# The first RMS norm of a two-block kernel: squares summed on VectorE, root and reciprocal on one column per 128 tokens

## The chip, the cores and the metric

One core of one Trainium2 chip runs the whole program in one launch. The metric is the device time in microseconds (us), the median of several runs. The kernel is written in a tile language: the source says which instructions exist and which data they use, and a planner decides in which order each engine gets them, by its own estimates of when each will be ready. Semaphores between the engines follow from the data and from the reuse of buffers.

## The reference, cut to what matters

There are 512 tokens of 1024 features and two blocks. Only the head of the first block is touched:

```
def rms_norm(x, w):
    xf = x.astype(jnp.float32)
    y = xf * lax.rsqrt(jnp.mean(xf * xf, axis=-1, keepdims=True) + EPS)
    return (y * w.astype(jnp.float32)).astype(x.dtype)
...
mod = jax.nn.silu(c) @ w_mod[l] + b_mod[l]
shift, scale, gate = jnp.split(mod, 3, axis=-1)
u = rms_norm(h, norm_w[l]) * (1.0 + scale[:, None, :]) + shift[:, None, :]
p = u @ w_in[l]
```

Behind it come attention, a convolution branch (GLU, depthwise convolution of width 31, layer norm, pointwise matmul), and the second block (RWKV mixer, memory attention, feed-forward).

## The kernel before, in words

Features lie on the 128 partitions and tokens on the free axis, so `x` comes as eight tiles of 128x512 (`xs[0..7]`, tile name `x`). RMS norm needs the sum of squares over features, which is a sum over the eight tiles and over the partitions.

Before the change, ScalarE (ACT) squares each tile into one of the four `tA` buffers, and TensorE (PE) multiplies it by a 128x128 matrix of 1/1024 (`ones`) into the bank `pj` of PSUM, adding the eight up. Every partition of `pj` then holds the mean square of each token, 128x512. ACT takes the root into `bs`, VectorE (DVE) the reciprocal, in place, again 128x512.

PE starts with `WARM` = 12 matmuls on zeros of 128x512 bf16 (`warm_up`), which have no use but to keep it busy. An ACT function table is loaded by an instruction of its own (ACT_TABLE_LOAD) where the next function isn't in the one loaded; a one-column Sqrt on `th` stands behind the Tanh to have Sqrt's table in place early.

The modulation comes from `mod_group`: eight matmuls of 32 rows (`pj<-modw,c`, eight 32-column weight loads of `c`), a copy `tA<-pj` on ACT, small matmuls `pv<-g,tA` of 2 columns, and on DVE the additions `c<-pv` that give `shift` and `A1`. `mod_pair(g)` serves the feature tiles 2g and 2g+1; the pair 0 is done in two halves. The groups 4 and 5 give the gate.

The loop `for j in range(KT)` then makes tile j of `u` (`apply_mod`: DVE multiplies `x` by `bs` into `tA`, ACT applies `A1` and `shift` once into `U` as the high part and once into `tA`, DVE forms the low part `U`), splits the weight tile `wr` into `wh` (ACT) and `wl` (DVE), and adds 18 matmuls of 128x512 to six accumulators (`accs`: two double banks `s`, two banks `pt`). I call these 18 matmuls group j. The first four of a group need only the high part of `u`. All weights and `w_mod` come through one DMA queue in the order of the source; `wr` has 2 buffers, `wl` 2, `wh` 3, `modw` 10.

Behind the loop come GLU (`hg<-tA,s`, `hg<-tA,pt`), the gate groups (`c<-pv`, 128x4), the convolution as 120 DVE instructions `hg<-hg,c` of low priority, a further projection `pj<-U`, and q and k/v projections.

A class `SumSq` that the changed code calls existed before, and a helper `norm_bs` uses it for the 256 context tokens.

Of the kernel before, what the change touches and what calls it, by code (L numbers as in the profile page):

```python
# [12 lines left out]
F32R = mybir.dt.float32r  # L13
# [3 lines left out]
AF = mybir.ActivationFunctionType  # L17
# [5 lines left out]
P = 128  # L23
S = 512
D = 1024
KT = 8
# [120 lines left out]
def rest(k, src, hi, lo):  # L147
    return k.V.tensor_tensor(out=lo, in0=src, in1=hi.bitcast(F32), op=ALU.subtract)
# [32 lines left out]
def mm3(k, ps, wh, wl, ah, al, first, last):  # L181
    mm = k.T.matmul
    mm(ps, wh, ah, start=first, stop=False)
    mm(ps, wh, al, start=False, stop=False)
    k.mm = mm(ps, wl, ah, start=False, stop=last)
    return k.mm
# [80 lines left out]
def bcast(k, r, n, tag):  # L267
    b = k.t(tag)
    for j in range(n):
        k.T.transpose(b[:, j * P:(j + 1) * P], r[:, j:j + 1].to_broadcast([P, P]), k.ident)  # L270
    return b
# [65 lines left out]
MODW = 10  # L337
LATER = 1500
CTX = (0, 2)
WARM = 12  # L340
ZG = (1, 0, 1, 1, 1, 0, 0, 0, 0, 0, 0)

def block1(k, I, st, h1d):
    A, V, T, G, Y = k.A, k.V, k.T, k.G, k.Y
# [7 lines left out]
    def warm_up(n):  # L352
        ps = k.t("pj")
        for _ in range(n):
            T.matmul(ps, warm[:, 0:P], warm, start=True, stop=True)

    xs = []
# [5 lines left out]
    sc, th = k.cal([16]), k.cal([16])  # L363
# [2 lines left out]
    cc = k.cal([KT, 32])  # L366
    G.memset(cc, 0.0)
    V.tensor_scalar(out=cc[:, :, 0:2], in0=sc.rearrange("p (i j) -> p j i", i=2), scalar1=0.5, scalar2=None, op0=ALU.mult)
    A.activation(th[:, 0:1], th[:, 0:1], AF.Sqrt, scale=0.0, bias=k.eps[1e-6])

    mark = [None] * 3
    warm_up(WARM)
    shift, A1 = k.cal([2, KT]), k.cal([2, KT])
# [4 lines left out]
    def mod_load(g, i):  # L378
        t = k.t("modw", [2, S])
        Y.dma_start(out=t, in_=I["w_mod"][g, i])  # L380
        return t
# [14 lines left out]
    def mod_pair(g, ts, e0=0, e1=2):  # L396
        cols = mod_group(ts, e0, e1)
        for e in range(e0, e1):
            j = 2 * g + e
            V.tensor_scalar(out=shift[:, :, j], in0=cols[:, 2 * e, :], scalar1=k.vec("b_mod", j), scalar2=None, op0=ALU.add)  # L400
            V.tensor_scalar(out=A1[:, :, j], in0=cols[:, 2 * e + 1, :], scalar1=bm1[:, j:j + 1],
                            scalar2=k.vec("norm_w", j), op0=ALU.add, op1=ALU.mult)
# [15 lines left out]
    def apply_mod(x, w, bs, i, j, hi, lo, vec=False):  # L418
        t = k.t("tA", [w])
        mark[1] = V.tensor_tensor(out=t, in0=x, in1=bs, op=ALU.mult)  # L420
        a_ap, s_ap = A1[:, i, j:j + 1], shift[:, i, j:j + 1]
        A.activation(hi, t, AF.Identity, bias=s_ap, scale=a_ap)
        if vec:
            V.tensor_scalar(out=t, in0=t, scalar1=a_ap, scalar2=s_ap, op0=ALU.mult, op1=ALU.add)
        else:
            mark[2] = A.activation(t, t, AF.Identity, bias=s_ap, scale=a_ap)
        V.tensor_tensor(out=lo, in0=t, in1=hi.bitcast(F32), op=ALU.subtract)
        return hi, lo

    ones = k.cal([P])  # L430
    G.memset(ones, 1.0 / D)
    ps = k.t("pj")
    for j in range(KT):
        sq = k.t("tA")
        A.activation(sq, xs[j], AF.Square)
        T.matmul(ps, ones, sq, start=j == 0, stop=j == KT - 1)
    bs = k.t("bs")
    A.activation(bs, ps, AF.Sqrt, bias=k.eps[1e-6])
    V.reciprocal(out=bs, in_=bs)
    a0, a1 = k.t("s", [2, S]), k.t("s", [2, S])  # L440
    accs = [a0[:, 0, :], a0[:, 1, :], a1[:, 0, :], a1[:, 1, :], k.t("pt"), k.t("pt")]
    us = []
# [9 lines left out]
    def raw_load(j):  # L452
        raw = k.t("wr", [1024])
        Y.dma_start(out=raw[:, :768], in_=I["w_start"][j])
        raws.append(raw)
# [5 lines left out]
    for j in range(KT):  # L461
        raw, wh, wl = raws[j], k.t("wh", [1024], F32R), k.t("wl", [1024], F32R)
        A.activation(wh[:, :768], raw[:, :768], AF.Copy)
        if j < 2:
            mod_pair(0, mods[0], j, j + 1)
        elif j % 2 == 0:
            mod_pair(j // 2, mods[j // 2])
        u = apply_mod(xs[j], S, bs, 0, j, k.t("U", dt=F32R), k.t("U", dt=F32R))
        us.append(u)
        rest(k, raw[:, :768], wh[:, :768], wl[:, :768])  # L470
        if j + 2 < KT:
            raw_load(j + 2)
        if j % 2 == 0 and j // 2 + 2 < 6:
            mods.append([mod_load(j // 2 + 2, i) for i in range(4)])
        for m in range(6):
            c = slice(m * P, (m + 1) * P)
            mm3(k, accs[m], wh[:, c], wl[:, c], u[0], u[1], j == 0, j == KT - 1)
# [42 lines left out]
    for g in range(4):  # L520
        wh, wl = W1.next()
        for kk in range(2):
            j = 2 * g + kk
            c = slice(kk * S, (kk + 1) * S)
            for t in range(4):
                tt = slice(t * P, (t + 1) * P)
                uh, ul = us[j]
                ps = q_ps[t // 2][:, t % 2, :]
# [18 lines left out]
    for t in (2, 3, 4, 5, 0, 1):  # L547
        ps = k.t("pt", [256])
# [278 lines left out]
    for m in range(KT):  # L827
        if m % 2 == 0:
            wh, wl = W1.next()
        ps = oacc[m]  # L830
# [654 lines left out]
def emit(tc, I, out, dbg=None, stages=("b1", "b2", "ff")):  # L1485
    k = K(tc, dbg)
    nc = tc.nc
    with ExitStack() as st:
        k.open(st, "g", dict(g=1, wr=2, wh=3, wl=2))
        setup(k, I)  # L1490
        h1d = nc.dram_tensor("h1d", (KT, P, S), F32, kind="Internal").ap()
        k.open(st, "H", dict(xa=6, xb=4, hg=16))
        p1 = ExitStack()
        k.open(p1, "p1", dict(c1=1, U=16, tA=4, kvs=6))
        k.open(p1, "p1m", dict(pj=1), PSUM)
        k.open(p1, "p1s", dict(s=2), PSUM)
        k.open(p1, "p1t", dict(pt=2), PSUM)
        k.open(p1, "p1v", dict(pv=1), PSUM)
        if "b1" not in stages:
            k.rest()  # L1500
        if "b1" in stages:
            nm = block1(k, I, p1, h1d)
        else:
            nm = Norm(k, "norm_mix_g", "hg", "xb")
            for j in range(KT):
                x = k.x()
                k.Y.dma_start(out=x, in_=I["xT"][:, j, :])
                k.Y.dma_start(out=h1d[j], in_=x)
                nm.add(j, x)
        p1.close()  # L1510
        k.nx = 0
        if "b2" in stages:
            k.open(st, "p2a", dict(c2=1, p=6, rk=4, v=2, z=2, bon=3, s8=6, nr=8))
            k.open(st, "p2m", dict(pj=2), PSUM)
            k.consts("c2", 1350)
            block2(k, I, nm, h1d, out)
# [95 lines left out]
```

## Time and profile before

| what | us |
|---|---|
| median of 3 runs | 1112.25 |
| lowest and highest | 1111.74, 1119.19 |
| the profiled execution, its own time | 1114.73 |
| its span, first to last instruction | 1112.9 |

The profiled execution spent 1.8 us outside its span. All times in the rows are counted from the span's start, in microseconds. The lines of the source are no help here, since most instructions are issued through one helper (L57); go by the names of the tiles. An arrow `out<-in` gives what is written and what is read. PE's float32 matmuls stand as two records, so eight of them are x16.

### The profile page before, as it was taken

What the parts mean: (1) busy time and instruction counts of PE and PEld (TensorE: products, weight loads), DVE (VectorE), ACT (ScalarE), POOL (GpSimd) and SP (SyncE); (2) the same over time, 40 slices, a digit from 0 to 9 for tenths busy, and PEclk for the clock granted to TensorE, in tenths of its full rate; (3) what the DMA queues carried; (4) which work ended last, traced back from release to release, by engine and by line L of the source; (5) the groups of instructions that cost most, each with busy time, mean ns of one, the idle gap of its engine ahead of it and who ended that gap; (6) DMA issues with size and microseconds to landing.
All of it is one profiled execution on the core that took longest, in us unless ns stands there. A gap on an engine that the chain in (4) does not pass through costs nothing.

```text
span 1112.9 us, 15943 instructions
## 1 busy us (share of the span) xinstructions
PE 1074.0 (97%) x6272; PEld 835.0 (75%) x6272; DVE 727.8 (65%) x1283; ACT 539.5 (48%) x987; POOL 55.4 (5%) x181
## 2 busy tenths in 40 slices
PE   8999989999999999999999989999999999999998
PEld 4668977666787777777777767768888888888887
DVE  3369999994675898897868897566444344344332
ACT  5445546774555556555556664565443133134110
POOL 0000000000010102121111101010000000000000
PEclk9999999999999999999999888999999999999999
DMA  9753221010353101101112112213233333333332
GB/s 340 285 175 105 64 71 58 1 39 20 95 182 109 57 23 37 39 26 33 39 39 62 57 58 67 77 38 95 94 95 98 98 104 99 95 95 95 95 123 85
DMA packets 32203, 96.46 MB, mean 87 GB/s; under 512 B 3456, under 2 KB 6272, under 8 KB 32128
## 3 DMA queue, kind: packets, MB, share of 16 engines
q1 hardware_dynamic: 32128, 95.45, 26.7%
q8 instruction: 49, 0.80, 0.3%
q14 instruction: 26, 0.21, 0.1%
HBM read 91.24 MB, written 4.19 MB: 86 GB/s over the span
## 4 chain that ended last, share of the span: by engine, by line
PE 84%; DVE 8%; ACT 5%; issue 1%; DMA 1%; POOL 0%; SPq 0%; ACTq 0%; DVEq 0%; POOLq 0%
PE pf L57 31%; PE pj L57 23%; PE s L57 9%; PE i L57 8%; PE pt L57 5%; PE pv L57 4%; PE y L57 3%; DVE wl L57 1%; DVE hg L57 1%; DVE p L57 1%; ACT tA L57 1%; ACT p L57 1%; DVE f L57 1%; ACT xb L57 1%; DVE c L57 1%
## 5 line engine op out<-in xcount | busy, mean ns | idle before, releaser
L57 ACT ACTIVATE wh<-wr 128x1024 fp32r<-128x1024 f32 (+1 forms) x132 | 137.5, 1042 | 182.8 <-PE pf L57 67.0
L57 DVE TENSOR_TENSOR wl<-wr,wh 128x1024 fp32r<-128x1024 f32 (+1 forms) x132 | 158.8, 1203 | 22.2 <-PE pt L57 10.0
L57 PE MATMUL pf<-A,wh 128*128 128x512 f32 x512 | 157.8, 389 | 0.0
L57 PE MATMUL pj<-hg,wh 128*128 128x512 f32 x448 | 155.8, 417 | 1.4 <-DVE x L57 0.9
L57 PEld LDWEIGHTS pf<-A,wh 128*128 128x128 f32 x512 | 96.0, 188 | 19.7
L57 ACT ACTIVATE f<-i 128x512 f16<-128x512 f32 (+1 forms) x132 | 71.3, 597 | 80.0 <-PE i L57 80.0
L57 PE MATMUL pf<-A,wl 128*128 128x512 f32 x256 | 99.6, 389 | 0.0
L57 DVE TENSOR_TENSOR x<-x,pf 128x512 f32<-128x512 f32 (+1 forms) x33 | 22.2, 672 | 113.9 <-PE pf L57 113.9
L57 PEld LDWEIGHTS pj<-hg,wh 128*128 128x128 f32 x448 | 81.0, 190 | 19.2 <-issue 3.0
L57 PE MATMUL pj<-hg,wl 128*128 128x512 f32 x224 | 90.5, 404 | 0.0
L57 DVE SCALAR_TENSOR_TENSOR hg<-hg,c 128x504 f32<-128x504 f32 (+14 forms) x120 | 84.9, 739 | 0.7 <-ACT hg L57 0.4
L57 PE MATMUL pf<-ff,wh 128*128 128x512 f32 (+1 forms) x272 | 79.7, 377 | 0.0
L57 PE MATMUL pf<-hg,wh 128*128 128x512 f32 x256 | 78.7, 389 | 0.0
L57 DVE SCALAR_TENSOR_TENSOR fr<-pf,r 128x512 f32<-128x512 f32 x32 | 22.1, 692 | 85.4 <-PE pf L57 82.1
L57 ACT ACTIVATE fr<-fr 128x512 f32<-128x512 f32 x32 | 20.2, 632 | 99.8 <-DVE fr L57 99.8
L57 PEld LDWEIGHTS <-f 128*128 128x128 f16 x720 | 47.5, 102 | 23.4 <-issue 14.7
L57 PE MATMUL i<-f 128*128 128x128 f16 x672 | 56.4, 226 | 3.5 <-DVE f L57 3.0
L57 PEld LDWEIGHTS pf<-ff,wh 128*128 128x128 f32 x272 | 50.1, 188 | 9.4
L57 PEld LDWEIGHTS pf<-A,wl 128*128 128x128 f32 x256 | 48.1, 188 | 10.0
L57 PEld LDWEIGHTS pf<-hg,wh 128*128 128x128 f32 x256 | 48.1, 188 | 9.9
L57 PE MATMUL pf<-ff,wl 128*128 128x512 f32 (+1 forms) x136 | 51.2, 376 | 0.0
L57 PE MATMUL pf<-hg,wl 128*128 128x512 f32 x128 | 49.8, 389 | 0.0
(312 smaller groups left out, 2111.4 us busy)
## 6 DMA issues: line engine op xcount, KB each, us to landing
wr<-w_ff SPq DMA_DIRECT2D x64, 512.0 KB, 3.5
modw<-w_mod SPq DMA_DIRECT2D x20, 512.0 KB, 7.4
wr<-rw_in SPq DMA_DIRECT2D x20, 512.0 KB, 3.5
wr<-w_in SPq DMA_DIRECT2D x10, 512.0 KB, 3.6
wr<-w_out SPq DMA_DIRECT2D x8, 512.0 KB, 3.5
wr<-w_start SPq DMA_DIRECT2D x8, 384.0 KB, 5.7
x<-xT SPq DMA_DIRECT2D x8, 256.0 KB, 5.1
modw<-w_mod SPq DMA_DIRECT2D x8, 256.0 KB, 6.1
```

The source lines that it names most:

```text
L57: r = f(*a, **kw)
```

## The change

The sum of squares goes through `SumSq`: ACT squares each tile as before, DVE adds the squares up tile by tile (seven additions, 128x512), and PE then makes only four matmuls of one column, `ss[:, t] = prev[:, t*128:(t+1)*128].T @ inv1k`, into a bank `pt` in place of `pj`. The result is 128x4, one token per partition. Root (ACT) and reciprocal (DVE) work on that. `bcast` spreads it to 128x512 with four 128x128 transposes into the second bank `pt`, and ACT copies it to `bs`. The first tile of `u` reads that PSUM bank itself. `WARM` goes from 12 to 22, and the one-column Sqrt reads a constant instead of `th`.

```diff
-WARM = 12
+WARM = 22
...
-    A.activation(th[:, 0:1], th[:, 0:1], AF.Sqrt, scale=0.0, bias=k.eps[1e-6])
+    A.activation(k.cal([1]), k.eps[1e-6], AF.Sqrt)
...
-    ones = k.cal([P])
-    G.memset(ones, 1.0 / D)
-    ps = k.t("pj")
+    ss = SumSq(k, "tA")
     for j in range(KT):
-        sq = k.t("tA")
-        A.activation(sq, xs[j], AF.Square)
-        T.matmul(ps, ones, sq, start=j == 0, stop=j == KT - 1)
+        ss.add(xs[j])
+    b0 = bcast(k, ss.rstd("pt", k.inv1k, 1e-6, k.cal([4])), 4, "pt")
     bs = k.t("bs")
-    A.activation(bs, ps, AF.Sqrt, bias=k.eps[1e-6])
-    V.reciprocal(out=bs, in_=bs)
+    A.activation(bs, b0, AF.Copy)
...
-        u = apply_mod(xs[j], S, bs, 0, j, k.t("U", dt=F32R), k.t("U", dt=F32R))
+        u = apply_mod(xs[j], S, bs if j else b0, 0, j, k.t("U", dt=F32R), k.t("U", dt=F32R))
```

The planner's order changes with it on PE, ACT and DVE as far as the convolution and the attention of the first block; beyond, each engine has the same instructions in the same order. Three places follow. In them `c_83` is the constant tile that the profile calls `c`.

On ACT, at the start of the program, the order before and then that of the change:

```order
L57 ACT_TABLE_LOAD
L57 ACTIVATE c_83<-g 128x16
L57 ACTIVATE tA<-x 128x512
L57 ACT_TABLE_LOAD
L57 ACTIVATE c_83<-c_83,g 128x1
L57 ACTIVATE tA<-x 128x512 x7
L57 ACTIVATE bs<-pj,g 128x512
```

```order
L57 ACT_TABLE_LOAD
L57 ACTIVATE c_83<-g 128x1
L57 ACT_TABLE_LOAD
L57 ACTIVATE c_83<-g 128x16
L57 ACTIVATE tA<-x 128x512 x8
L57 ACT_TABLE_LOAD
L57 ACTIVATE c_83<-pt,g 128x4
L57 ACTIVATE tA<-pj 128x256
```

The one-column Sqrt (`c_83<-g 128x1`) has moved ahead of the Tanh (128x16), and a third table load stands between the last square and the root `c_83<-pt,g`.

On PE, behind the warm-up matmuls and up to the first matmuls of group 0, before and then with the change:

```order
L57 MATMUL pj<-tA,c_83 128x512 x8
L57 MATMUL pj<-modw,c_83 32x256 x8
L57 MATMUL pv<-g,tA 128x2 x2
L57 MATMUL pj<-modw,c_83 32x256 x8
L57 MATMUL pv<-g,tA 128x2 x2
L57 MATMUL s<-U,wh 128x512 x2
```

```order
L57 MATMUL pj<-modw,c_83 32x256 x2
L57 MATMUL pt<-g,tA 128x1 x4
L57 MATMUL pj<-modw,c_83 32x256 x6
L57 MATMUL pt<-g,c_83 128x128 x4
L57 MATMUL pv<-g,tA 128x2 x2
L57 MATMUL pj<-modw,c_83 32x256 x4
L57 MATMUL s<-U,wh 128x512 x2
```

The eight matmuls of 512 columns are gone, four of one column and four transposes have come, and half of the second modulation half (x8 before, x4 now) has moved behind the first matmuls of group 0, and with it the `pv` that gives tile 1 its factors.

On PE, between two groups of the loop: before, the modulation of tiles 6 and 7 (the first x8) with all its steps stood between group 5 and group 6; now the x8 at the head of the second piece is that modulation and stands ahead of group 4, and its `pv` behind group 5.

```order
L57 MATMUL pt<-U,wl 128x512
L57 MATMUL pj<-modw,c_83 32x512 x8
L57 MATMUL pv<-g,tA 128x2 x4
L57 MATMUL pj<-modw,c_83 32x512 x8
L57 MATMUL s<-U,wh 128x512 x2
L57 MATMUL pt<-U,wh 128x512 x2
```

```order
L57 MATMUL pt<-U,wl 128x512
L57 MATMUL pj<-modw,c_83 32x512 x3
L57 MATMUL pv<-g,tA 128x2 x4
L57 MATMUL pj<-modw,c_83 32x512 x8
L57 MATMUL s<-U,wh 128x512 x2
L57 MATMUL pt<-U,wh 128x512 x2
```

The x3 and the `pv` ahead of it belong to tiles 4 and 5, whose modulation is now finished only behind group 3.

## Rows read from the trace of the kernel before

**Rows 1.** The page: busy time by engine, and the chain that ended last
```profile
PE 1074.0 (97%) x6272; PEld 835.0 (75%) x6272; DVE 727.8 (65%) x1283; ACT 539.5 (48%) x987; POOL 55.4 (5%) x181
...
PE 84%; DVE 8%; ACT 5%; issue 1%; DMA 1%; POOL 0%; SPq 0%; ACTq 0%; DVEq 0%; POOLq 0%
```

**Rows 2.** Windows (stretch, PE, weight loads, DVE, ACT, POOL busy, granted clock, DMA)
```profile
5.50:14.20 8.70, 7.94 (x19) 2.95 (x17) 0.00 (x0) 5.79 (x10) 0.00 (x0) 1.00 1.03 359
...
75.00:90.00 15.00, 15.00 (x68) 12.40 (x67) 14.93 (x25) 5.28 (x11) 0.00 (x0) 1.00 0.24 70
```

**Rows 3.** The chain in order of time, 5 to 21 us: start, us, what
```profile
14.21 0.70 ACT bs L57
...
18.43 0.69 DVE tA L57
...
19.15 0.82 ACT U L57
...
20.01 0.73 PE s L57 x2
```

**Rows 4.** Timeline of the start: start, us, engine, instruction, idle before
```profile
10.85 0.63 ACT L57 ACTIVATE tA<-x 128x512 f32<-128x512 f32 x1
...
14.93 3.35 DVE L57 RECIPROCAL bs<-bs 128x512 f32<-128x512 f32 x1 [11.32 <-ACT bs L57]
...
16.59 0.61 PE L57 MATMUL pv<-g,tA 128*128 128x2 f32 x4 [0.56 <-ACT tA L57]
...
18.24 0.27 DVE L57 TENSOR_SCALAR c<-pv,c,g 128x2 f32<-128x2 f32 x1
```

**Rows 5.** Groups by shape, 75 to 110 us: count, busy us, mean ns, idle before
```profile
L57 ACT ACT_TABLE_LOAD x1 | 1.3, 1283 | 0.0
...
L57 PE MATMUL pj<-g,tA 128*128 128x1 f32 x4 | 0.5, 228 | 0.0
...
L57 PE MATMUL pv<-g,c 128*128 128x128 f32 x2 | 0.4, 272 | 0.0
...
L57 ACT ACTIVATE c<-pj,g 128x2 f32<-128x2 f32 x1 | 0.3, 263 | 0.0
L57 DVE RECIPROCAL c<-c 128x2 f32<-128x2 f32 x1 | 0.2, 167 | 0.0
```

**Rows 6.** The DMA issued at 8.07 us: count, KB, us to landing
```profile
modw<-w_mod SPq DMA_DIRECT2D x1, 256.0 KB, 5.7
```

**Rows 7.** The chain in order of time, 48 to 75 us
```profile
48.03 2.72 PE s L57 x12
...
52.11 1.93 PE pj L57 x16
...
54.05 0.61 ACT tA L57
...
54.70 1.07 PE pv L57 x8
...
59.59 2.58 PE s L57 x10
...
69.45 2.88 PE pj L57 x16
```

**Rows 8.** Windows around 70 us, columns as in Rows 2
```profile
66.80:68.40 1.60, 0.35 (x2) 0.00 (x0) 1.34 (x2) 1.60 (x4) 0.00 (x0) 1.00 1.00 410
...
70.10:73.60 3.50, 3.50 (x17) 1.23 (x9) 1.47 (x5) 1.75 (x3) 0.00 (x0) 0.51 0.37 136
```

**Rows 9.** Timeline: weight loads of the warm-up, then two steps on DVE
```profile
4.80 0.15 PEld L57 LDWEIGHTS <-bs 128*128 128x128 bf16 x1 [0.28 <-issue]
5.23 0.35 PEld L57 LDWEIGHTS <-bs 128*128 128x128 bf16 x2 [0.28 <-issue]
...
67.41 1.23 DVE L57 TENSOR_TENSOR wl<-wr,wh 128x1024 fp32r<-128x1024 f32 x1 [0.26 <-ACT wh L57]
...
74.41 0.16 DVE L57 TENSOR_TENSOR c<-pv,g 128x4 f32<-128x4 f32 x1 [2.83 <-PE pv L57]
```

## The prediction, made before the changed kernel was run

> **What bounds the kernel now.** First the page. PE is busy for 97% of the span and holds 84% of the chain that ended last [rows 1], so over the whole program a gain must shorten what PE does or waits for. The change touches only the head. The windows show why a shift there would be felt at the end: between 75 and 90 us PE and DVE are both busy throughout [rows 2], so neither has slack in which a later or earlier head could vanish, and what the loop's end gains or loses is handed on.
>
> Then the chain in order of time at the head. The last square ends at 10.85 + 0.63 = 11.48 [rows 4]. PE is still working off its eight matmuls of 512 columns, so the root starts only at 14.21; it takes 0.70, the reciprocal over 128x512 runs from 14.93 to 18.28 [rows 3, 4], the first product `tA` ends at 19.12, `U` at 19.97, and group 0 starts at 20.01 [rows 3]. From the last square it is 8.5 us.
>
> Last the chain in the loop. The pace inside a group is 2.72/12 = 0.227 us a matmul, so the 8 x 18 matmuls take 32.7 us. From 59.59 the last 32 come without a gap and end at 59.59 + 7.3 = 66.9 [rows 7]. The loop thus lasts 46.9 us, and 14.2 of it lie between the groups. The largest of those gaps opens at 52.11: modulation matmuls, the copy on ACT, `pv`, DVE and ACT, until 59.59.
>
> **The change part by part, 1: the way to group 0.** Step by step with full clock: the last of seven additions follows the last square and costs what the like-shaped product does, 0.69 [rows 3]: 12.2. The other six run between squares, on a DVE that has nothing else there; behind their waits nothing is queued but the reciprocal. Four one-column matmuls: two of them (x4) take 0.5 [rows 5], so 1.0: 13.25. Root 0.26: 13.55; reciprocal 0.17: 13.75 [rows 5]. Ahead of the transposes in PE's queue stand six modulation matmuls, whose last tile lands at 8.07 + 5.7 = 13.8 [rows 6]; with some 0.4 for them, 14.2. Four transposes at 0.4 for two less their overlap [rows 5], 0.6: 14.8. `pv` 0.61: 15.4 [rows 4]. The two small DVE steps, 0.4 with the 0.27 of the second [rows 4]: 15.85. Product 0.69, `U` 0.82 [rows 3]: 17.4. Group 0 starts **2.6 us earlier** than 20.0.
>
> At nothing I cost: the product that reads PSUM in place of SBUF (if it were 0.1 slower, 0.1 on this path); the bank `pt` shared with the accumulators, whose first use follows the product anyway; the copy to `bs`, covered by the steps that wait for `pv`; and the matmuls of `pj`, which no longer wait for root and sums. The third table load starts at 11.48, when the last square leaves ACT, and lasts 1.28 [rows 5], to 12.76; the addition and the sums cover it, until 13.25. Without that cover it would cost its 1.28.
>
> In the trace a load has no idle time before it and the next instruction none behind it [rows 5]. The Trainium skill (page "ScalarE: Activation LUTs", section "What ACT_TABLE_LOAD costs") adds a drain and counts about 2.66 us for every switch of set. By that the root would start at 14.1 and group 0 about 0.6 to 0.9 later; this case's 1.28 with no idle decides for nothing.
>
> **2: the order in the loop.** I walk the new order with the same durations and list the gaps between groups. A gap behind modulation matmuls is: copy 0.61, `pv` 1.07 [rows 7], DVE 0.4, `U` 0.82 [rows 3], small hand-overs, plus what is left of the matmuls; where a group's first four run ahead, the low part of `u` follows about 1.6 after the high one (a step like `U` and one like the product). Group 0, first four to the rest: 0.65. To group 1: the end of the modulation's second half and its whole tail stand behind group 0 now: 2.75. In group 1: 0.65. To group 2: 3.8. In group 2: 0.6. To group 4: tiles 4 and 5 get their factors only behind group 3, with the 1.93 of the next modulation [rows 7] filling part: 4.4. To group 6, whose modulation is done early: 2.3, where it was 7.5. In group 6: 0.75. Sum 15.9, against 14.2. The loop ends at 17.4 + 32.7 + 15.9 = 66.0, **0.9 earlier** than 66.9: of the 2.6 won ahead, the order gives back 1.7. The loads keep their order in the one queue, and don't come into it: by this walk the last weight tile is issued near 48.6 and needed after 58.
>
> **3: the clock.** Before, sums fill the time behind the warm-up: PE is busy 7.94 of 8.70 us from 5.5 to 14.2, and the granted clock stays 1.00 [rows 2]. Now these are gone. The warm-up's weight loads come 0.43 apart until 5.2, then two within 0.35 [rows 9], so 22 of them end near 8.2; then PE has nothing until about 11.5, and only short pieces until 17.4. What such a hole does, the trace shows at 68 us: PE was busy 0.35 of 1.60, and from 70.1 to 73.6 the granted clock was 0.51, half of 2.4 GHz, though PE was then busy all the time [rows 8]; a modulation of x16 took 2.88 there, 1.93 at full clock [rows 7]. So I expect the low level from about 12. At the start PE had worked from 1.4 without a hole when its matmuls drew closer at 5.2; the new dense work begins at about 18, so I put the rise at about 22. The price: 2.2 us of sums, transposes and `pv` at half clock, between 0 and 2.2 more, since weight loads and latencies fill most of it, so 0.8; the first four of group 0, 0.9 more; of its other fourteen about five, 1.1 more; less 0.8 of gaps in which PE waits for `u` anyway. Sum **2.0 later**; nothing if the clock stays up, 4 if it rises only at 26.
>
> The Trainium skill ("TensorE: Matmul & The Clock Gate", section "What's actually happening") says that "the default state is throttled, and activity releases the throttle". The trace agrees (0.51 at 70.1); by that rule the forecast's case stands above the rival with a full clock.
>
> **4: behind the loop.** DVE waits 2.83 us for the last gate `pv`, with small `qc` work ahead of it. Now a weight split `wl` (1.23 [rows 9]) and a second convolution step stand there in place of four small ones, and two projection matmuls no longer precede that `pv` on PE. At least 0, at most the whole 2.8; I take most of the split that now fits in, **1.0 earlier**. It counts because DVE is full from there on [rows 2].
>
> **The sum.** -0.9 + 2.0 - 1.0 = 0.1, that is nothing: span 1112.9, execution 1114.7. The median of the runs lies 2.4 below the profiled execution; on it, **1112.3 us**.
>
> **Rivals.** (a) The clock holds through the hole, since 22 warm-ups carry it: -0.9 - 1.0 = -1.9, 1110.4; and where the order gives nothing back either, -2.6 - 1.0 = -3.6, 1108.7. For it: the clock did survive short holes between 14 and 20. Against it: this one is longer, and that at 68 was enough. (b) Slower: low clock until 26. Every microsecond of dense work at the low level costs a half, so it decides from about 24, where the forecast's gains are used up: -0.9 + 4 - 0 = +3.1, 1115.4. For it: groups 0 and 1 are broken by gaps in the new order, so dense work may come late. Against it: the low stretch at 70 ended after 3.5 us [rows 8]. (c) The change doesn't do all it says: the early Sqrt, meant to have the table in place, is queued ahead of the Tanh and so a load comes back in front of the root. That it happens is certain from the order; if its 1.28 isn't covered, the sum is +1.4, 1113.6.
>
> **How the numbers follow.** Forecast 0.55, (a) 0.22, (b) 0.18, (c) 0.05; the predicted time is the forecast's. The range reaches from the full case of (a) to a little over (b), since the order differs until the convolution ends and one more low stretch like that at 70 costs about 1: 1108.6 to 1116.0. A change of 1% is 11 us, about what a measurement of this kernel can tell from none; no case comes near it. Faster by over 1% 0.01, within 1% 0.97, slower by over 1% 0.02, for mechanisms that I don't see.
>
> **What the profile will show.** Group 0's first `s<-U,wh` at 17.4 to 19; a reciprocal of 128x4 of about 0.17 near 14; a table load of 1.28 at 11.5 with the root behind the sums, not behind the load; a granted clock near 0.5 in a good part of 12 to 22; the loop's last matmul between 65 and 69; a gap of under 3 ahead of group 6 and one over 4 ahead of group 4; a gate wait on DVE under 2 near 73. I am wrong if group 0 starts before 17 or after 20, if the clock never falls before 25, or if the difference grows between 90 us and the end, where orders are the same.

## The result, and the profile after

The changed kernel's median is 1120.29 us over 22 runs (1114.41 to 1123.74), that of the kernel before, timed beside it, 1115.24 over 22. The ratio is 1.0052, with a 95% interval of 1.0037 to 1.0066: slower by half a per cent, inside the 1% that the prediction called no change, and outside its range (1108.6 to 1116.0). The median on which the prediction stood, 1112.25, came from three runs and lies 3 us low; on it the ratio gives 1118.0, still outside.

The profiled execution took 1123.74 us, the highest of its runs, with a span of 1121.8. Its windows at the start, columns as in [rows 2]:

```profile
5.50:14.20 8.70, 4.78 (x21) 2.00 (x19) 4.85 (x7) 5.63 (x8) 0.00 (x0) 0.98 1.02 334
14.20:20.00 5.80, 5.67 (x34) 3.48 (x33) 1.28 (x5) 2.04 (x5) 0.00 (x0) 0.50 1.07 382
20.00:30.00 10.00, 8.72 (x38) 4.88 (x38) 3.43 (x6) 3.15 (x5) 0.00 (x0) 0.79 1.00 398
```

The hole behind the warm-up is there (PE busy 4.78 of 8.70 us, where [rows 2] has 7.94), and the clock stands at 0.50 from 14.2 to 20, half of 2.4 GHz.

The chain of the changed kernel in order of time (start, us, what), answering to [rows 3, 7]:

```profile
13.67 1.66 PE pt L57 x8
15.32 1.85 PE pj L57 x12
17.17 1.05 PE pt L57 x4
18.22 0.66 PE pv L57 x4
...
19.31 0.60 DVE tA L57
...
19.94 0.82 ACT U L57
...
20.80 1.22 PE s L57 x2
...
31.61 0.97 PE pj L57 x2
...
49.81 1.05 PE pj L57 x6
...
50.88 0.61 ACT tA L57
...
51.53 1.05 PE pv L57 x8
52.59 1.85 PE pj L57 x16
54.44 0.66 PE s L57 x2
...
73.92 1.37 PE pt L57 x6
```

Group 0 starts at 20.80 (20.01 before), and the loop ends at 75.3, where the trace of the kernel before has its last group matmul end at 67.2. Two things are to be seen. Ahead of group 0 the sums are followed by 1.85 of modulation matmuls before the transposes. Ahead of group 4 stands a whole sequence, 49.81 to 54.44: the end of a modulation (x6), the copy, `pv`, and eight matmuls of the next modulation, before the first `s`.

The timeline of the changed kernel has the small steps, answering to [rows 4, 5, 9]:

```profile
12.53 1.28 ACT L57 ACT_TABLE_LOAD   x1
15.36 0.27 ACT L57 ACTIVATE c<-pt,g 128x4 f32<-128x4 f32 x1 [1.55 <-PE pt L57]
...
15.66 0.18 DVE L57 RECIPROCAL c<-c 128x4 f32<-128x4 f32 x1 [2.04 <-ACT c L57]
...
81.23 0.16 DVE L57 TENSOR_TENSOR c<-pv,g 128x4 f32<-128x4 f32 x1 [1.05 <-PE pv L57]
```

The reciprocal fell from 3.35 to 0.18; the load of 1.28 is covered, since the root waits for PE; and the wait for the last gate is 1.05 instead of 2.83.

### The profile page after: what moved, and what is told of

Read it like the earlier page. It is cut to its first block, busy times and chain, and to the rows that moved or that the text cites. A ratio compares the mean times of both kernels' runs of the same rounds, so it can differ in the third digit from the quotient of the medians.

```text
span 1121.8 us, 15954 instructions
## 1 busy us (share of the span) xinstructions
PE 1079.1 (96%) x6278; PEld 835.0 (74%) x6278; DVE 729.7 (65%) x1290; ACT 541.5 (48%) x989; POOL 55.2 (5%) x180
## 4 chain that ended last, share of the span: by engine, by line
PE 82%; DVE 9%; ACT 4%; DMA 2%; issue 1%; POOL 0%; SPq 0%; ACTq 0%; DVEq 0%; POOLq 0%
PE pf L57 31%; PE pj L57 22%; PE s L57 9%; PE i L57 8%; PE pt L57 5%; PE pv L57 4%; PE y L57 3%; DVE hg L57 2%; DVE wl L57 1%; DVE p L57 1%; ACT xb L57 1%; ACT p L57 1%; ACT tA L57 1%; DVE f L57 1%; DVE c L57 1%
## 5 line engine op out<-in xcount | busy, mean ns | idle before, releaser
L57 PEld LDWEIGHTS pf<-A,wh 128*128 128x128 f32 x512 | 96.0, 188 | 19.9
L57 DVE SCALAR_TENSOR_TENSOR hg<-hg,c 128x503 f32<-128x503 f32 (+14 forms) x120 | 84.9, 737 | 0.4
L57 ACT ACTIVATE fr<-fr 128x512 f32<-128x512 f32 x32 | 20.2, 632 | 100.2 <-DVE fr L57 100.2
```

What stands on the lines that cost most here:

```text
L57: r = f(*a, **kw)
```

## The experiments

For the order on PE I write G for a group's matmuls, m and M for modulation matmuls of 256 and 512 columns, v for `pv`, S for the sums, T for the transposes, with the number of instructions. Behind the warm-ups the two kernels have

```
before   S8 m8 v2 m8 v2 G4 M4 G32 M4 v4 M8 G4 v4 G68 M8 v4 M8 G36
changed  m2 S4 m6 T4 v2 m4 G4 m3 G14 m1 v2 M4 G4 M1 G14 M3 v4 M4 G4 M1 G32 M3 v4 M8 G36 v4 M5 G4 M3 G32
```

The old kernel's eight S are its sums over 128x512. I call these the old and the new order. Theory A: the new order is the loss. Rival B: the low clock at the start is.

**First four: order or clock, by the source.** e1 chains the matmuls of the changed kernel in the old order, with its own place for the sums; e2 keeps the new order and fills the hole with 46 warm-ups, e3 does both, and e4 is the kernel before with 22 warm-ups.

```diff
-WARM = 22
+WARM = 46
+PLAN = "m2 S4 m6 T4 v2 m8 v2 G4 M4 G32 M4 v4 M8 G4 v4 G68 M8 v4 M8 G36"
...
+                if self.chain:
+                    self.k.after(r, self.chain[-1])
+                self.chain.append(r)
```

> The changed kernel with the loop's order on TensorE written out as the kernel before has it (modulation tails placed as there), the new norm and the 22 warm-ups kept. Theory A (the new order costs most of the loss: 18.3 us of gaps between the groups instead of 13.1): the half clock stays from about 14 to 24 and group 0 still starts near 20.8, but the loop ends 4 to 5 us earlier than the 75.3 of the changed kernel, near 70.5; time against before within +0.1% (-0.2 to +0.3). Rival B (the low clock at the start costs most, the order little): loop end above 73.5, time still some +0.4%.

> The changed kernel's order on TensorE pinned down, with 46 warm-up matmuls instead of 22, so that they last until about the one-column sums. Theory A (order): the low stretch near 14 to 24 goes, group 0 starts near 18.5 instead of 20.8, the loop ends near 72.5, since the gaps stay near 18; time +0.2%. Rival B (clock): group 0 near 18 and the loop's end near 70 or less, time within 0.1% of before.

> Both at once: the order of the kernel before in the loop and 46 warm-ups with the new norm. If the two causes add (A and B each hold a part): group 0 near 18, loop end near 66 to 67, time -0.1 to -0.2% against before. If a third cause is at work behind the loop (something the new norm leaves behind), the time stays above that of before by 0.3% though the loop ends no later.

> The kernel before with 22 warm-ups in place of 12 and nothing else; the planner then writes another order, with five modulation matmuls ahead of a group's first four and three behind them, as in the changed kernel. Theory A: the order is what counts, so the gaps in the loop grow by 1 to 4 us against before though the norm is the old one and the clock stays full; loop end 68 to 71 where before has 66.9, time +0.1 to +0.3%. Rival B: no hole in front, so no loss: loop end 66 to 67.5, time within 0.1%.

Ratios: e1 1.0037 (1.0013 to 1.0061), e2 1.0066 (1.0040 to 1.0091), e3 1.0034 (1.0012 to 1.0057), e4 1.0048 (1.0024 to 1.0071). Loop ends: 74.4, 78.5, 72.2, 68.4. Taken by its own condition, e1 spoke for B; e2 ended later than either theory had it, and e3 later than its 66 to 67. And by e4 ten warm-ups alone would be the whole change: they cost half a per cent with a loop that ends about 1 later. That made me compare the orders behind the loop. In all four the planner had written PE's order anew as far as 294 us on the clock of the trace of before; that of the changed kernel itself last differs near 161 us. So these four don't separate A from B: each changed a second thing.

**Next four: the order fixed on every engine.** Behind the norm both kernels issue the same instructions in the source. So I took the order of either kernel as a list, for all five engines from the norm to the end, and bound the instructions to it:

```diff
+    for eng, seq in order.items():
+        for a, b in zip(seq, seq[1:]):
+            tc.add_manual_dep(seen[start + b], seen[start + a].name, SCHED, reason="pinned")
```

> The kernel before with 22 warm-ups, and on every engine the order of the kernel before for all that stands behind the norm (in the earlier run of this change the planner rewrote the order up to 300 us). Theory A (the order that the planner writes is the loss): without the rewriting nothing or little is lost, the loop ends between 66.9 and 69 (the ten added matmuls hold the sums up by at most 2), time within 0.1% of before. Rival B (the ten warm-ups themselves cost): loop end 69 or later and +0.3% or more.

> The changed kernel (new norm, 22 warm-ups) with the order of the kernel before, fixed on every engine from the norm to the end; sums two modulation matmuls into the first eight, as in the changed kernel. Theory A: the half clock stays (about 14 to 24 or later) and group 0 starts at 21 to 22, the loop ends near 71 to 74, but the stretch from 90 to 300 us keeps the order of before, so the time is +0.1% (0 to +0.3). Rival B (the low clock is the loss): loop end 74 or later, +0.4%.

> The kernel before (old norm, 12 warm-ups) with the changed kernel's order fixed on every engine behind the norm. Theory A (order): the clock stays full at the start and group 0 starts near 20.0, but the gaps between the groups sum to about 18 instead of 13 and the loop ends at 71 to 73, 4 to 6 later than 66.9; time +0.4%. Rival B (clock): loop end below 69, time within 0.1%.

> The changed kernel with 46 warm-ups and otherwise its own order, fixed on every engine. No granted clock of one half between 12 and 20. Theory B (clock): group 0 starts near 18.5, the loop ends near 71 or earlier, 4 earlier than the 75.3 of the changed kernel, time +0.1%. Theory A (order): group 0 starts earlier, but the groups wait for their factors all the same; loop end 73 to 75, time +0.4%.

Two more belong to this table: g1, the kernel before once more, and g2, the last corner.

> The kernel before once more: its own order, only written out; the instructions are the same. It asks whether its clock at the start is the same in every execution. If the full clock up to 70 us of the first profile is a property of the kernel: no low stretch before 70, group 0 near 20.0, loop end near 67. If it varies from one execution to the next (the old norm with the new order had a low stretch from 17.2 to 24.0 with the same start): a low stretch between 17 and 28, loop end 68 to 70.

> The changed kernel's norm with 46 warm-ups and the order of the kernel before, fixed on every engine; it differs from the earlier run with 46 warm-ups in the order alone. Theory A (order): no low clock at the start, the second half of the first modulation stands ahead of group 0, whose tiles land near 18, so group 0 starts at 19.5 to 20.4; the gaps are those of before, loop end 66.5 to 67.5, 5 earlier than with the new order (71.9); time -0.1% against before (-0.3 to +0.1). Rival: the new norm leaves some other delay; loop end 70 or later.

| kernel | norm, warm-ups, order | group 0 | loop end | ratio (95%) |
|---|---|---|---|---|
| before, g1 | old, 12, old | 20.0, 20.5 | 67.2, 67.9 | 1 |
| f1 | old, 22, old | 23.0 | 72.4 | 1.0002 (0.9976 to 1.0027) |
| f2 | new, 22, old | 22.9 | 72.3 | 1.0002 (0.9975 to 1.0028) |
| g2 | new, 46, old | 20.2 | 67.6 | 1.0001 (0.9977 to 1.0025) |
| f3 | old, 12, new | 19.9 | 74.6 | 1.0061 (1.0040 to 1.0081) |
| changed | new, 22, new | 20.8 | 75.3 | 1.0052 (1.0037 to 1.0066) |
| f4 | new, 46, new | 18.9 | 71.9 | 1.0027 (1.0009 to 1.0044) |

With the old order, norm and warm-ups change nothing that can be measured, which is to within about 0.25%. With the new order every kernel is slower, the one with the old norm too. The cleanest pair is f2 and the changed kernel, which differ in the order alone: 1.0002 against 1.0052, with intervals that lie apart. Theory A holds. B holds a part: f4, whose clock stays at 1.00 throughout the start, is 0.25% below the changed kernel (the two intervals overlap by 0.07%), and its loop ends 3.3 earlier. In time neither part can be called the larger (0.27% is left in f4 for the order, 0.25% goes to the clock); under the old order the low clock of f1 and f2 cost nothing that can be measured. At full clock the loop takes 71.9 - 18.9 = 53.1 us in the new order (f4) and 67.6 - 20.2 = 47.4 in the old (g2): 5.7 more. The window and the chain of f4:

```profile
14.20:20.00 5.80, 4.75 (x37) 2.61 (x36) 2.45 (x6) 3.83 (x7) 0.00 (x0) 1.00 1.07 382
```

```profile
14.61 1.01 PE pj L60 x12
...
18.87 0.73 PE s L60 x2
...
28.26 0.97 PE pj L60 x2
...
46.45 1.05 PE pj L60 x6
...
47.52 0.60 ACT tA L60
...
48.17 1.05 PE pv L60 x8
49.23 1.85 PE pj L60 x16
51.08 0.66 PE s L60 x2
...
70.58 1.37 PE pt L60 x6
```

Ahead of group 4 these are the rows of the changed kernel to 0.01 us, 3.36 earlier.

The misses are f1's loop end (66.9 to 69 expected, 72.4 measured) and f3, whose clock was to stay full and fell (0.75 over 14.2 to 20), with a loop end of 74.6 where 71 to 73 was expected. In f1's and f2's profiles the clock falls at the start (0.57 and 0.66 over 20 to 30 us) and the loop ends 5 later than before, yet the time is that of before. Part of it is made good behind the loop. Their last instructions come 0.7 and 0.6 earlier than in the trace of before, because that trace has low stretches near 288, 384 and 504 us that theirs lack. Whether that is so in every execution isn't shown: a single profile's shift at 70 us is not yet the time. The same caution holds for the new order: that it costs time is measured, that the 5.7 us in the loop are this time is argued from profiles.

**Which rows of the new order.** g3 and g4 have an order of my own in the loop, h1 the same without the gates' modulations (the plan of h1 is shown; g3 adds `M8 G4 v4` twice in groups 6 and 7). h2 moves only the late modulations of the new order into the group before; h4 is h2 with each modulation's matmuls kept together.

```
h1  m2 S4 m6 T4 v2 G4 m8 G8 v2 G10 M8 G4 v4 G14 M8 G4 v4 G32 M8 G4 v4 G64
h2  m2 S4 m6 T4 v2 m4 G4 m3 G14 m1 v2 M4 G4 M1 G2 M3 G6 v4 G6 M4 G4 M1 G20 M3 G6 v4 G10 M8 G8 v4 G24 M5 G4 M3 G32
h4  m2 S4 m6 T4 v2 m4 G4 m4 G14 v2 G4 M8 G8 v4 G10 M8 G26 v4 G10 M8 G8 v4 G28 M8 G32
```

> The new norm with 46 warm-ups and an order of my own on TensorE in the loop: each modulation stands right behind the first four matmuls of the last group ahead of its use, its pv four matmuls later, and both gates' modulations inside groups 6 and 7 instead of behind the loop; on the other engines the loop is left to the planner, and behind it stands the changed kernel's order. Theory A (the loss is waits for factors behind late modulations): the gaps in the loop fall to 10 to 13 with the modulations in them, group 0 at 18.9, loop end 63 to 66, and the first projection follows it within 2 us instead of 7; time -0.3 to -0.7% against before. Rival (the loop is bound by the arrival of the modulation tiles, whatever the order): loop end 67 or later, time within 0.2%.

> The same order of my own with the old norm and 12 warm-ups: what the norm is worth once the order no longer hides it. Group 0 at 19.5 to 20.5 instead of 18.9 (the reciprocal over 128x512 is back), loop end 64 to 67, about 1 later than with the new norm, and 1 to 2 more where the clock falls at the start; time -0.2 to -0.5% against before. If the norm is worth its forecast 2.6 us, the distance between the two is over 0.2%.

> The new norm with 46 warm-ups and the order of my own in the loop, but both gates' modulations behind the loop again. If VectorE sets the pace behind the loop and starts with the loop's last matmul, what counts is the loop's end and not when the first projection starts: without 5.3 us of gate work the loop ends at 64 to 66 (71.5 with it), VectorE's convolutions start 1 to 3 earlier than in the kernel before, and the time falls by 0.1 to 0.3%. If the early gates were no hindrance: no difference to the earlier run of this order (0.9992).

> The changed kernel with 46 warm-ups and its own order, in which only the modulations ahead of groups 2 and 4 and the pv ahead of group 6 are moved 6 to 12 group matmuls forward, into the group before (and the next modulation from ahead of group 4 to behind its first four). If those waits are the loss: the gaps ahead of groups 2, 4 and 6 (4.5, 5.0 and 2.9 with the same 46 warm-ups) shrink to under 2 each, the loop ends near 66 instead of 71.9, and the time falls from +0.27% to between -0.1 and +0.1%. If the factors come late for another reason (tiles, ScalarE), the gaps move into the groups and the loop ends at 70 or later.

> The previous kernel (the waits moved into the groups) with each modulation's matmuls kept together: in fours for the first, in eights for the others, where that kernel cuts them into pieces of 4, 1 and 3 or of 5 and 3. In its trace a piece of one (two records) takes 1.05, of three 1.06, of four 1.07 and of eight 1.92, so a cut set costs its time again. If that is the rest of the loss: the pieces fall from 3.2 to 1.95 twice and from 3.0 to 1.95 once, the first modulation loses one piece of 0.56, together some 4 us; loop end 67.5 to 69 instead of 72.3, time within 0.15% of before instead of +0.41%. If the price is per matmul and the pieces only fill waits that remain: loop end 71 or later, time +0.3% or more.

| kernel | group 0 | loop end | loop | ratio (95%) |
|---|---|---|---|---|
| f4 | 18.9 | 71.9 | 53.1 | 1.0027 (1.0009 to 1.0044) |
| h2 | 19.6 | 72.3 | 52.7 | 1.0041 (1.0014 to 1.0068) |
| h4 | 19.0 | 66.2 | 47.2 | 1.0001 (0.9971 to 1.0030) |
| g3 | 20.0 | 71.5 | 51.4 | 0.9992 (0.9968 to 1.0016) |
| g4 | 20.3 | 72.2 | 51.8 | 0.9998 (0.9975 to 1.0021) |
| h1 | 20.0 | 65.4 | 45.4 | 0.9971 (0.9941 to 1.0002) |

h2 felled theory A in its first form. The waits ahead of groups 2, 4 and 6 went (no gap there is over 2.2), and the loop ended at 72.3 all the same. Its timeline shows what had taken their place:

```profile
30.29 1.05 PE L60 MATMUL pj<-modw,c 128*32 128x512 f32 x2
...
31.93 1.06 PE L60 MATMUL pj<-modw,c 128*32 128x512 f32 x6
...
36.76 1.07 PE L60 MATMUL pj<-modw,c 128*32 128x512 f32 x8
...
50.52 1.92 PE L60 MATMUL pj<-modw,c 128*32 128x512 f32 x16
```

Two records are one matmul. One, three and four modulation matmuls take the same 1.05 to 1.07 us, eight take 1.92. Their outputs go to four strips of 32 partitions, four at a time. A modulation cut into 4, 1 and 3 so costs 3.2 where a whole one costs 1.9. The Trainium skill ("TensorEngine Tiling (Array Packing)", section "Key Properties") states that different tiles of the array can load weights and multiply in parallel, and that a change of the tiling mode drains the engine. The trace agrees with the parallel part by these rows; a drain would fit the 0.36 us that PE's weight loads stand idle before such a piece in f4 (19.99 us), which no run here takes apart.

h4 keeps the pieces whole and is back at 66.2 and at the time of before. Its chain:

```profile
27.06 1.85 PE pj L60 x16
...
34.30 1.85 PE pj L60 x16
...
45.62 1.85 PE pj L60 x16
...
64.82 1.37 PE pt L60 x6
```

From h2 to h4 the loop lost 5.5 us and the time 0.40%, or 4.5 us, against the 4 that the pieces add up to. The two intervals (1.0014 to 1.0068 and 0.9971 to 1.0030) overlap, so it is the loop that shows the gain, and the time only agrees with it. Two other things differ. The clock over 20 to 30 us was 0.86 in h2's profile and 1.00 in h4's; from its first to its last start group 0 takes 6.2 us in h2 and 4.8 in h4 (and in f4, at full clock), so 1.4 of the 5.5 is the clock, and 4.1 is left for the pieces. And 8 rows on VectorE and 4 on ScalarE stand otherwise, since in the loop the planner still orders these engines; what they are worth isn't shown.

Another rival is the new order behind the loop, which differs as far as 161 us. From 78 us on, h4, g3, g4 and h1 all have the changed kernel's order, and none is slower than the kernel before (1.0001, 0.9992, 0.9998 and 0.9971). So the loss isn't there.

g3 expected a gain of 0.3 to 0.7% and has none that can be measured: its first projection starts 2.9 earlier than before (71.30 against 74.23), but the sixteenth step of the convolution on VectorE starts 1.7 later (89.48 against 87.78). The loop ends of g3 and g4, 71.5 and 72.2, miss what was expected (63 to 66 and 64 to 67): the gates' modulations stand inside the loop, and h1 without them ends at 65.4, which also speaks against g3's rival of late modulation tiles. Its timeline on VectorE, then that of h1:

```profile
69.08 0.16 DVE L60 TENSOR_TENSOR c<-pv,g 128x4 f32<-128x4 f32 x1 [6.94 <-PE pv L60]
...
70.67 1.28 DVE L60 SCALAR_TENSOR_TENSOR hg<-tA,s 128x512 f32<-128x512 f32 x2 [0.26 <-ACT tA L60]
72.49 0.69 DVE L60 SCALAR_TENSOR_TENSOR hg<-tA,pt 128x512 f32<-128x512 f32 x1 [0.53 <-ACT tA L60]
...
74.58 2.67 DVE L60 SCALAR_TENSOR_TENSOR hg<-hg,c 128x497 f32<-128x497 f32 x4
```

```profile
63.31 0.69 DVE L60 SCALAR_TENSOR_TENSOR hg<-tA,s 128x512 f32<-128x512 f32 x1 [5.06 <-ACT tA L60]
...
72.64 0.17 DVE L60 TENSOR_TENSOR c<-pv,g 128x4 f32<-128x4 f32 x1 [2.29 <-PE pv L60]
72.74 2.68 DVE L60 SCALAR_TENSOR_TENSOR hg<-hg,c 128x497 f32<-128x497 f32 x4
```

In g3 both gates' modulations lie inside the loop, so VectorE's GLU, which needs the loop's sums, begins at 70.67. With them behind the loop (h1) it begins at 63.31, and the convolution at 72.74 instead of 74.58. That is not the 1 to 3 ahead of the kernel before that was expected: the sixteenth step starts at 87.65, against 87.78 there. h1 is the best version found: 0.29% below the kernel before, with an interval that just touches no change, and clearly below the changed kernel (1.0052).

g3 and g4 differ in the norm and the warm-ups and not measurably in time (0.9992, 0.9998). That doesn't settle what the norm alone is worth: the 46 warm-ups of g3 run until 14.11 and the sums start only at 14.73, 1.2 later than in f4, and group 0 starts only 0.3 earlier than in g4. In f4 it starts 1.1 to 1.6 ahead of the old kernel.

## Why the prediction was wrong

**The way to group 0: 2.6 earlier forecast, 0.8 later measured.** Right were the reciprocal, the product that reads PSUM (0.68 in both timelines), the hidden copy, and the load of 1.28 behind the addition and the sums. The time at which the sums can start was wrong. f4 shows it at full clock, where group 0 starts at 18.87, 1.5 after the forecast's 17.4:

```profile
8.96 3.41 ACT L60 ACTIVATE tA<-x 128x512 f32<-128x512 f32 x5 [1.72 <-DMA x<-xT]
9.63 3.88 DVE L60 TENSOR_TENSOR tA<-tA 128x512 f32<-128x512 f32 x5 [1.49 <-ACT tA L60]
```

The squares wait 1.72 for a tile of `x` and end at 12.37, not at 11.48; in the changed kernel they wait 1.57 and end at 12.51. The 11.48 came from one execution: in g1, the same kernel as before, they end at 12.36, and the old norm doesn't feel it, since its root waits for PE's eight matmuls and starts at 14.2 to 14.3 in both traces. And five additions take 3.88, 0.80 from one to the next where the squares come 0.70 apart, so the last ends 1.1 behind the last square instead of 0.7: at 13.5, 1.3 later than the forecast. From there on f4 takes 5.4 to group 0, and the forecast 5.2. In the changed kernel the low clock comes on top: the six modulation matmuls that stand behind the sums on PE take 1.85 (1.01 in f4) and hold the transposes back until 17.17, 1.3 after the reciprocal, where the forecast had 0.45. At full clock group 0 starts 1.1 to 1.6 before the old kernel. With the old order even that is gone (g2, 20.2 against 20.0 and 20.5), because the modulation's second half stands ahead of group 0.

**The order in the loop: this step failed.** The forecast summed the gaps to 15.9 against 14.2, a loss of 1.7. At full clock the loop is 53.1 - 32.7 = 20.4 beyond its matmuls in f4, against 47.4 - 32.7 = 14.7 in g2: a loss of 5.7. The large waits of the walk were nearly right; the single matmuls in them were not. The walk took the 1.93 of eight modulation matmuls [rows 7] as a price per matmul, and let single ones fill waits for nothing. In fact a single one takes as long as four (0.97 in the chain). Gap by gap in f4 (start to start less the pace of 0.227): in groups 1, 2 and 6 1.1 each instead of 0.65, 0.6 and 0.75; to groups 1, 2, 4 and 6 3.1, 4.3, 4.7 and 2.7 instead of 2.75, 3.8, 4.4 and 2.3. These make 2.8 of the missing 4.5; 1.2 more are eleven places right behind a break where the next matmul follows after 0.34 instead of 0.227. (The 7.5 that the prediction gives for the old gap ahead of group 6 reaches to that group's fifth matmul; to its first it is 6.1.) That the pieces, with the waits that they prolong, are the loss is shown in the loop by h4: with whole ones it takes 47.2, as in g2, and the time, 1.0001 (0.9971 to 1.0030), can't be told from before.

**The clock: right in kind, too small.** The warm-up ended at 9.1 instead of 8.2; the clock fell, at 13.9 instead of 12, and rose at 24.2 instead of 22. Between f4 and the changed kernel 1.9 are lost ahead of group 0, where I had 0.8, and 1.4 inside it, where I had 1.2. The price is 3.3 at the loop's end (f4 against the changed kernel), 0.25% or 2.8 us in time, where I had put 2.0 with bounds of 0 and 4.

**Behind the loop: right.** The gate's wait shrank by 1.8. The loop ends 8.1 later than before, the first projection starts 6.8 later (81.05 against 74.23): 1.3 won, 1.0 forecast.

**The sum.** Forecast was 0.1. Measured at the first projection it is +6.8 in the profiles, and 5.1 between the medians. Rival (b) had the right sign, and its low clock did last to 24, but it named the clock as the cause, and at the loop's end the clock is 3.3 where the order is 5.7. No rival was an order that costs several microseconds. The third rival (a load ahead of the root, not covered) was right that it comes back and wrong that it might cost. (The 0.6 to 0.9 that the prediction gives for a root at 14.1 come out at some 0.45 by its own steps.)

**The difference behind 90 us.** Two of the prediction's signs of being wrong came true: group 0 started after 20, and the difference grew behind 90 us. On VectorE it stays between 6.8 and 8.3 until 270, sinks to 4.0 near 420 and ends at 8.6, with low stretches at other places in the two traces (288, 384 and 504 us before, 458 and 512 with the change, among others). What sets these places is open.

## What to carry to other kernels

Where a planner writes the order, a change at the head is a change of every later row that the planner touches: compare the orders engine by engine first, and to learn what the edit itself is worth, fix the old order and run the edit alone. When walking an order, price each piece by a row of that very size: the modulation matmuls, which run side by side on strips of the array, cost the same for one as for four here (1.05 and 1.07 us), so keep such a set together. Before work is moved ahead, ask which engine starts with the end of the stage: filling PE's loop with gate work (g3 against h1) brought the projections forward by 1.2 and the convolution back by 1.8, and gained nothing that can be measured. And a time at which data arrive, read from one execution, is one value of several (11.48 and 12.36 here): read a second trace of the same kernel before a forecast starts from it.

## What the runs showed of the hardware

One modulation matmul of 32 output rows and 512 columns takes 1.05 us, and so do four; eight take 1.92. I had expected about 0.24 each.

The clock at the start depends on more than the hole behind the warm-up. With the old norm, 12 warm-ups and the old order it stayed full until 70 us in one profile and until 155 in another; with the new order and the same start it was 0.75 over 14.2 to 20 and 0.80 over 20 to 30 (f3). With 46 warm-ups it was 1.00 from 14.2 to 30 in g2, f4 and h4, and 0.83 over 20 to 30 in g3 and h1. How busy PE was from 14.2 to 20 doesn't sort these cases: 2.71 of 5.80 us in f3, 3.44 in f1 and 3.62 in h1, which fell, and 3.52 in the kernel before, which didn't. What does is open.
